# Two masked groups of a chain in one visit over four PSUM banks, and a matrix product cut to 96 rows and columns

## The chip, the cores and the metric

The kernel runs on one core of one Trainium2 chip. The metric is the device time of one execution in microseconds, from runs on the chip. A profile is one further execution, recorded by the hardware profiler; its span runs from the first to the last instruction of the program.

## The reference

One hybrid decoder layer in float32, with 256 tokens of width 2048: a SwiGLU feed-forward, a mixer (sliding-window attention beside RWKV-7 time mixing), cross-attention into a memory of 256 rows, a second feed-forward and a final RMSNorm. What is changed lies in the time mixing. For each of 16 heads of width 64 it is a recurrence over the tokens:

```python
def step(S, inp):
    r_t, w_t, k_t, v_t, a_t, b_t = inp
    sa = jnp.einsum('bhij,bhj->bhi', S, a_t)
    S = S * w_t[:, :, None, :] + sa[..., None] * b_t[:, :, None, :] + v_t[..., None] * k_t[:, :, None, :]
    return S, jnp.einsum('bhij,bhj->bhi', S, r_t)
```

A step needs the state that the step before left. The kernel works instead in chunks of 128 tokens: within a chunk it solves a triangular system, and between the two chunks it hands on the state.

## The kernel before

Weight products fill TensorE from the first to the last microsecond. A weight tile of 128x512 is split into a high and a low part (`hi` on ScalarE, line 365; `lo` on VectorE, line 366), and each product is three matmuls of 512 columns (lines 442 to 444). The two parts are made up to two items ahead (`AHEAD`); an item is 12 matmuls in the mixer.

All other work of the mixer is written as Python generators in an `Interleave`. After each group of six product matmuls `bg.tick()` lets every active generator emit its next step, up to its `yield`. So the steps of a chain stand in the queues of the engines between the weight products, one step per tick; `idle(n)` is n ticks in which a generator emits nothing. The framework then orders the instructions and sets all semaphores: an instruction that finds no free buffer is put later, and an instruction may go ahead of one that was emitted earlier.

The generator `pairs(h, q)` is the chain. Each of its four instances (h and q are 0 or 1) carries two pairs of heads through the two chunks c = 0 and 1, and at most two instances run at a time. In order of steps:

- `masked` (line 1315) multiplies keys, removal keys and receptances (lines 1326 and 1327; the two heads of a pair stand on partitions 0 to 63 and 64 to 127, each goes to a bank of its own) and applies a triangular mask on VectorE (line 1332). It is called three times: for the first two kinds of c = 0 (`mk`), one tick later for the third kind of both chunks (`later`), and after `sa` for the first two kinds of c = 1 (`mk_next`).
- `u` (line 1363) is the right side of the system; N (line 1378) is the product of two precomputed parts of its matrix: `x` holds the inverses of the four 32x32 diagonal blocks, `rr` what lies below those blocks. `nt` is N copied to SBUF (line 1383).
- `stage` (line 1387) does one product and its copy to SBUF. `v0` is x times u; then three products with N: `v1` = v0 + N v0, `w` = N v1, `sa` = v1 + N w. They share one bank `vb`, and `v1` and `sa` add onto what `v0` left there. `rr` holds nothing in rows 0 to 31 and nothing in columns 96 to 127; so the first 32 columns of `nt` and its rows 96 to 127 are zero.
- The output `y` and, for c = 0, the state `s0`.

PSUM has eight banks: three `acc` for the weight products, three `mm` and two `tr`. In this part of the kernel `mm` holds `vb` of each chain and, for a short time, the transposes `bk`; `tr` holds the masked products, `u`, N, `y`, and the transposes and sums of other generators (`finish`, `values`, `shifted`).

POOL (GpSimd) fills and loads `x` and `rr` (`inverse_blocks`, lines 1299 to 1305), loads `g2` in `finish` (lines 1467 to 1469) and stores `gr` (line 1524).

Of the kernel before, what the change touches and what calls it, by code (L numbers as in the profile page):

```python
# [15 lines left out]
P = 128  # L16
# [120 lines left out]
def decoder_layer(ctx: ExitStack, tc: tile.TileContext, a: dict, out: bass.AP):  # L137
    nc = tc.nc
    act, dve, pool, pe = nc.scalar, nc.vector, nc.gpsimd, nc.tensor
# [26 lines left out]
    def tr():  # L166
        return ps.tile([P, 512], F32, tag="tr", name="tr", bufs=2)
# [5 lines left out]
    def idle(n):  # L173
        for _ in range(n):
            yield
# [94 lines left out]
    for entry in weight_plan(a):  # L270
# [4 lines left out]
        w, k0, nk, c0, n = entry  # L275
# [5 lines left out]
        for k in range(k0, k0 + nk, 2 * KU):  # L281
            u = len(units)
# [528 lines left out]
    with tc.tile_pool(name="f1", bufs=1, reuse_waits="tile") as sp:  # L811
        aligned(sp)
        at["pool"] = sp
        x = sp.tile([P, 2, D], F32, name="x")
# [58 lines left out]
    with tc.tile_pool(name="mx", bufs=1, reuse_waits="tile") as sp:  # L873
# [3 lines left out]
        def t4(name, shape=(P, 4, T), dt=F32):  # L877
            return sp.tile(list(shape), dt, tag="t4", name=name, bufs=N4)
# [427 lines left out]
            xb[h, c] = x, r  # L1306

        rows = [slice(64 * e, 64 * e + 64) for e in range(2)]
        ek = dict(skip_group_check=True)
        yq = {}  # L1310

        def small(name, tag="sm", bufs=6):
            return sp.tile([P, 2, P], F32, tag=tag, name=name, bufs=bufs)

        def masked(h, js, which):


            sides = ((aa[h], at_[h]), (aa[h], rt[h]), (bt[h], rt[h]))
            b = [tr() for _ in range(2)]
            for i, (m, c) in enumerate(which):  # L1320
                cs_ = slice(c * P, (c + 1) * P)
                x1, x2 = sides[m]
                for k, j in enumerate(js):
                    o = (2 * i + k) * P
                    for e, r in enumerate(rows):
                        pe.matmul(  # L1326
                            b[e][:, o : o + P], x1[r, j, cs_], x2[r, j, cs_], start=True, stop=True
                        )
            t = t4("mk", (P, 2, 4, P))
            mask = mask3[:, :2] if which[0][0] == 0 else mask3[:, 1:]  # L1330
            for e in range(2):
                dve.tensor_tensor(
                    t[:, e].rearrange("p (m k) t -> p m k t", m=2),
                    b[e][:].rearrange("p (m k t) -> p m k t", m=2, k=2),
                    mask.unsqueeze(2).to_broadcast([P, 2, 2, P]), ALU.mult,
                )
            return t

        def pairs(h, q):
            yield from wait_for("inverse")  # L1340
            yield from wait_for(f"ready{h}")
            js = (2 * q, 2 * q + 1)
            y = yq[h, q] = sp.tile([P, 2, T], F32, tag="yq", name="yq", bufs=3)
            if q == 0:
                for c in range(2):
                    inverse_blocks(h, c)

            yield from idle(4 + 4 * q)
            ah, bh, kh, rh = at_[h], bt[h], aa[h], rt[h]
            s0 = later = None  # L1350
            for c in range(2):
                cs_ = slice(c * P, (c + 1) * P)
                if c == 0:
                    mk = masked(h, js, ((0, 0), (1, 0)))
                    yield
                    later = masked(h, js, ((2, 0), (2, 1)))
                    yield
                vp = [vtok[h][:, c, j * P : (j + 1) * P] for j in js]
                x, rr = xb[h, c]
                b = tr()  # L1360
                for k, j in enumerate(js):
                    for e, r in enumerate(rows):
                        pe.matmul(
                            b[:, k * P : (k + 1) * P][:, r], mk[:, e, k, :], vp[k][:, r],
                            start=k + e == 0, stop=c == 0, **ek,
                        )
                    if c:
                        pe.matmul(
                            b[:, k * P : (k + 1) * P], ah[:, j, cs_], s0[:, k, :], start=False,
                            stop=True, **ek,  # L1370
                        )
                u = small("u")
                act.copy(u[:], b[:, : 2 * P].rearrange("p (k f) -> p k f", k=2))
                b = tr()
                for k, j in enumerate(js):
                    for e in range(2):
                        o = (2 * k + e) * P
                        pe.matmul(
                            b[:, o : o + P], rr[:, 4 * e + j, :], x[:, 4 * e + j, :],
                            start=o == 0, stop=True, **ek,  # L1380
                        )
                nt = sp.tile([P, 4, P], F32, tag="nt", name="nt", bufs=2)
                act.copy(nt[:], b[:].rearrange("p (k t) -> p k t", k=4))
                yield
                vb = mm()

                def stage(lhs, rhs, o, first, name):
                    for k in range(2):
                        for e, r in enumerate(rows):
                            pe.matmul(  # L1390
                                vb[:, (o + k) * P : (o + k + 1) * P][:, r], lhs(k, e), rhs[:, k, r],
                                start=first and k + e == 0, stop=True, **ek,
                            )
                    s = small(name)
                    act.copy(
                        s[:], vb[:, o * P : (o + 2) * P].rearrange("p (k f) -> p k f", k=2)
                    )
                    return s

                v0 = stage(lambda k, e: x[:, 4 * e + js[k], :], u, 0, True, "v0")  # L1400
                if c == 0:
                    b = mm()
                    for k, j in enumerate(js):
                        for i, z in enumerate((bh, kh)):
                            o = (2 * k + i) * P
                            pe.transpose(b[:, o : o + P], z[:, j, cs_], ident[:])
                    bk = sp.tile([P, 4, P], F32, tag="bk", name="bk", bufs=2)
                    act.copy(bk[:], b[:].rearrange("p (x f) -> p x f", x=4))
                yield
                v1 = stage(lambda k, e: nt[:, 2 * k + e, :], v0, 0, False, "v1")  # L1410
                yield
                w = stage(lambda k, e: nt[:, 2 * k + e, :], v1, 2, False, "w")
                yield
                sa = stage(lambda k, e: nt[:, 2 * k + e, :], w, 0, False, "sa")
                yield
                if c == 0:
                    mk_next = masked(h, js, ((0, 1), (1, 1)))
                    yield
                b = tr()
                if c:  # L1420
                    for k, j in enumerate(js):
                        pe.matmul(
                            b[:, k * P : (k + 1) * P], s0[:, k, :], rh[:, j, cs_], start=k == 0,
                            stop=False, **ek,
                        )
                for k in range(2):
                    o = slice(k * P, (k + 1) * P)
                    for e, r in enumerate(rows):
                        pe.matmul(
                            b[r, o], vp[k][:, r], mk[:, e, 2 + k, :], start=c + k == 0, stop=False,  # L1430
                            **ek,
                        )
                    for e, r in enumerate(rows):
                        pe.matmul(
                            b[r, o], sa[:, k, r], later[:, e, 2 * c + k, :], start=False, stop=True,
                            **ek,
                        )
                if c == 0:
                    for k in range(2):
                        bs = b[:, (2 + k) * P : (3 + k) * P]  # L1440
                        pe.matmul(bs, bk[:, 2 * k, :], sa[:, k, :], start=False, stop=False, **ek)
                        pe.matmul(bs, bk[:, 2 * k + 1, :], vp[k], start=False, stop=True, **ek)
                act.copy(y[:, :, cs_], b[:, : 2 * P].rearrange("p (k t) -> p k t", k=2))
                if c == 0:
                    s0 = small("s0", "s0", 2)
                    for k, j in enumerate(js):
                        dve.scalar_tensor_tensor(
                            s0[:, k, :], b[:, (2 + k) * P : (3 + k) * P], dec[h][:, j : j + 1],
                            bdup[:], ALU.mult, ALU.mult,
                        )  # L1450
                    mk = mk_next
                yield
            for j in js:
                bg.seen.add(f"y{4 * h + j}")
# [104 lines left out]
        for n in range(4):  # L1559
            s = t4("x2", (P, 2, 512))  # L1560
# [193 lines left out]
```

## Time and profile before

| | |
|---|---|
| time, median of 3 runs | 2233.55 us (2233.27 to 2233.90) |
| the profiled execution's own time | 2234.97 us |
| its span, first to last instruction | 2233.2 us |
| granted TensorE clock | 0.999 |
| TensorE busy (matmuls; weight loads) | 2218.3 us; 1825.6 us |
| VectorE, ScalarE, GpSimd busy | 1828.1, 1248.2, 116.6 us |
| HBM | 208 GB/s over the span |
| the changed code runs | 1099 to 1252 us |

In the lines of the profile PE is TensorE's matmuls, PEld its weight loads, DVE is VectorE, ACT ScalarE, POOL GpSimd. A group shows its line of the program, engine, operation, output and inputs, for TensorE rows*columns of the array, then the shape of the operand that is read, and the count. One fp32 product of the program is two matmuls and two weight loads in the trace. Matmuls overlap, so the spacing of their starts says more than how long one lasts. In lists of one line's instructions the three numbers are shortest, median and longest, in ns. In the chain of waits and the timeline the first number is the start in us and the second the length.

### The profile page before, as it was taken

What the parts mean: (1) busy time and instruction counts of PE and PEld (TensorE: products, weight loads), DVE (VectorE), ACT (ScalarE), POOL (GpSimd) and SP (SyncE); (2) the same over time, 40 slices, a digit from 0 to 9 for tenths busy, and PEclk for the clock granted to TensorE, in tenths of its full rate; (3) what the DMA queues carried; (4) which work ended last, traced back from release to release, by engine and by line L of the source; (5) the groups of instructions that cost most, each with busy time, mean ns of one, the idle gap of its engine ahead of it and who ended that gap; (6) DMA issues with size and microseconds to landing.
All of it is one profiled execution on the core that took longest, in us unless ns stands there. A gap on an engine that the chain in (4) does not pass through costs nothing.

```text
span 2233.2 us, 28140 instructions
## 1 busy us (share of the span) xinstructions
PE 2218.3 (99%) x10520; PEld 1825.6 (82%) x10520; DVE 1828.1 (82%) x2366; ACT 1248.2 (56%) x1626; POOL 116.6 (5%) x181
## 2 busy tenths in 40 slices
PE   9999999999999999999999999999999999999998
PEld 7888888888888877788888888888888888888876
DVE  7999989898989477877657656547999999999997
ACT  7555555555556468544444546556665565655654
POOL 0000000000001001200221030001000000000000
PEclk9999999999999999999999999999999999999999
DMA  8565566556556545677768688658575576556563
GB/s 303 193 211 199 189 208 201 194 189 212 202 189 199 173 134 153 188 236 208 225 202 277 200 262 282 188 160 279 195 251 194 193 245 207 203 208 220 198 240 137
DMA packets 231561, 466.02 MB, mean 209 GB/s; under 512 B 15521, under 2 KB 17921, under 8 KB 231425
## 3 DMA queue, kind: packets, MB, share of 16 engines
q1 hardware_dynamic: 222256, 438.08, 59.3%
q0 software_dynamic: 7648, 23.52, 3.4%
q10 hardware_dynamic: 1520, 2.63, 0.3%
q8 instruction: 82, 1.34, 0.3%
q14 instruction: 55, 0.44, 0.1%
HBM read 440.49 MB, written 23.59 MB: 208 GB/s over the span
## 4 chain that ended last, share of the span: by engine, by line
PE 91%; DVE 4%; DMA 3%; issue 1%; ACT 1%; SPq 0%; POOL 0%; POOLq 0%; ACTq 0%; DVEq 0%
PE acc L442 18%; PE acc L443 18%; PE acc L444 18%; PE mm L442 8%; PE mm L443 8%; PE mm L444 8%; PE tr L443 2%; PE tr L630 2%; PE tr L442 2%; PE tr L444 2%; DVE lo L366 2%; PE mm L1390 1%; DMA raw<-in_ffn_w_up_dram 1%; PE tr L1326 1%; PE mm L949 0%
## 5 line engine op out<-in xcount | busy, mean ns | idle before, releaser
L365 ACT CAST hi<-raw 128x1024 fp32r<-128x1024 f32 (+1 forms) x768 | 754.9, 993 | 685.6 <-PE acc L444 500.9
L366 DVE TENSOR_TENSOR lo<-raw,hi 128x1024 fp32r<-128x1024 f32 (+1 forms) x768 | 882.5, 1152 | 298.7 <-ACT hi L365 296.2
L442 PE MATMUL acc<-hi,xhi 128*128 128x512 f32 (+1 forms) x1134 | 446.9, 395 | 2.3 <-ACT hi L365 0.8
L443 PE MATMUL acc<-lo,xhi 128*128 128x512 f32 (+1 forms) x1134 | 440.5, 389 | 0.8 <-DVE lo L366 0.8
L444 PE MATMUL acc<-hi,xlo 128*128 128x512 f32 (+1 forms) x1134 | 440.2, 388 | 0.0
L442 PEld LDWEIGHTS acc<-hi,xhi 128*128 128x128 f32 x1134 | 212.8, 188 | 49.4 <-issue 3.7
L443 PEld LDWEIGHTS acc<-lo,xhi 128*128 128x128 f32 x1134 | 213.1, 188 | 44.9 <-DVE lo L366 2.1
L444 PEld LDWEIGHTS acc<-hi,xlo 128*128 128x128 f32 x1134 | 213.0, 188 | 44.2 <-issue 1.3
L373 ACT CAST thi<-raw 128x1024 fp32r<-128x1024 f32 x192 | 200.3, 1052 | 75.2 <-DVE raw L396 50.6
L374 DVE TENSOR_TENSOR tlo<-raw,thi 128x1024 fp32r<-128x1024 f32 x192 | 232.1, 1217 | 0.8 <-ACT thi L373 0.2
L442 PE MATMUL mm<-hi,xhi 128*128 128x512 f32 x402 | 156.6, 389 | 0.0
L443 PE MATMUL mm<-lo,xhi 128*128 128x512 f32 x402 | 156.5, 389 | 0.0
L444 PE MATMUL mm<-hi,xlo 128*128 128x512 f32 x402 | 156.4, 389 | 0.0
L444 PE MATMUL acc<-hi,hlo 128*128 128x512 f32 x372 | 145.4, 391 | 0.0
L443 PE MATMUL acc<-lo,hhi 128*128 128x512 f32 x372 | 145.3, 391 | 0.0
L442 PE MATMUL acc<-hi,hhi 128*128 128x512 f32 x372 | 145.0, 390 | 0.0
L442 PEld LDWEIGHTS mm<-hi,xhi 128*128 128x128 f32 x402 | 75.5, 188 | 16.3 <-ACT hi L365 0.5
L443 PEld LDWEIGHTS mm<-lo,xhi 128*128 128x128 f32 x402 | 75.5, 188 | 15.8
L444 PEld LDWEIGHTS mm<-hi,xlo 128*128 128x128 f32 x402 | 75.5, 188 | 15.7
L443 PEld LDWEIGHTS acc<-lo,hhi 128*128 128x128 f32 x372 | 69.8, 188 | 14.4
L444 PEld LDWEIGHTS acc<-hi,hlo 128*128 128x128 f32 x372 | 69.9, 188 | 14.1
L442 PEld LDWEIGHTS acc<-hi,hhi 128*128 128x128 f32 x372 | 69.9, 188 | 14.1
(400 smaller groups left out, 3548.7 us busy)
## 6 DMA issues: line engine op xcount, KB each, us to landing
raw<-in_ffn_w_down_dram SPq DMA_DIRECT2D x88, 1024.0 KB, 5.2
raw<-in_ffn_w_gate_dram SPq DMA_DIRECT2D x84, 1024.0 KB, 5.2
raw<-in_ffn_w_up_dram SPq DMA_DIRECT2D x78, 1024.0 KB, 6.1
raw<-in_w_in_dram SPq DMA_DIRECT2D x136, 512.0 KB, 3.7
raw<-in_w_out_dram SPq DMA_DIRECT2D x32, 512.0 KB, 4.8
raw<-sums SPq DMA_DIRECT2D x20, 512.0 KB, 6.3
raw<-in_w_proj_attn_dram SPq DMA_DIRECT2D x16, 512.0 KB, 4.3
raw<-in_w_proj_rwkv_dram SPq DMA_DIRECT2D x16, 512.0 KB, 6.0
```

What stands on the lines that cost most here:

```text
L365: at["hi"] = act.copy(hi[:, s], raw[:, s])
L366: at["lo"] = dve.tensor_tensor(lo[:, s], raw[:, s], f32(hi[:, s]), ALU.subtract)
L373: act.copy(hi[:], v[:])
L374: dve.tensor_tensor(lo[:], v[:], f32(hi[:]), ALU.subtract)
L442: pe.matmul(o, xh, hi, start=first, stop=False, **how)
L443: pe.matmul(o, xh, lo, start=False, stop=False, **how)
L444: pe.matmul(o, xl, hi, start=False, stop=last, **how)
L630: pe.transpose(b[:, o : o + P], tok[:, t, col : col + P], ident[:])
L1326: pe.matmul(b[e][:, o : o + P], x1[r, j, cs_], x2[r, j, cs_], start=True, stop=True)
L1390: pe.matmul(vb[:, (o + k) * P : (o + k + 1) * P][:, r], lhs(k, e), rhs[:, k, r], start=first and k + e == 0, stop=True, **ek,)
```

## The change

`masked` is split into `scores`, which does the matmuls into banks of a given ring, and `masked`, which applies the mask. For c = 0 the first and the second group are now emitted in the same step: the first into the two `tr` banks, the second into two `mm` banks; the four masks follow, and two idle ticks stand where the two steps were. The third group is as before.

N is computed for 96 rows (weights `rr` in 96 columns) and 96 columns (`x` without its first 32); the first 32 columns of `nt`, which the copy no longer writes, are set to zero by a memset on POOL. The products with N (`lower`) contract over 96 partitions in place of 128, and `w` is computed for 96 output rows only, since what follows reads no more of it.

```diff
@@ -1306,17 +1306,16 @@
             xb[h, c] = x, r
 
         rows = [slice(64 * e, 64 * e + 64) for e in range(2)]
+        low = slice(0, 96)
         ek = dict(skip_group_check=True)
         yq = {}
 
         def small(name, tag="sm", bufs=6):
             return sp.tile([P, 2, P], F32, tag=tag, name=name, bufs=bufs)
 
-        def masked(h, js, which):
-
-
+        def scores(h, js, which, bank):
             sides = ((aa[h], at_[h]), (aa[h], rt[h]), (bt[h], rt[h]))
-            b = [tr() for _ in range(2)]
+            b = [bank() for _ in range(2)]
             for i, (m, c) in enumerate(which):
                 cs_ = slice(c * P, (c + 1) * P)
                 x1, x2 = sides[m]
@@ -1326,8 +1325,10 @@
                         pe.matmul(
                             b[e][:, o : o + P], x1[r, j, cs_], x2[r, j, cs_], start=True, stop=True
                         )
+            return b
+
+        def masked(b, mask):
             t = t4("mk", (P, 2, 4, P))
-            mask = mask3[:, :2] if which[0][0] == 0 else mask3[:, 1:]
             for e in range(2):
                 dve.tensor_tensor(
                     t[:, e].rearrange("p (m k) t -> p m k t", m=2),
@@ -1351,10 +1352,11 @@
             for c in range(2):
                 cs_ = slice(c * P, (c + 1) * P)
                 if c == 0:
-                    mk = masked(h, js, ((0, 0), (1, 0)))
-                    yield
-                    later = masked(h, js, ((2, 0), (2, 1)))
-                    yield
+                    first = scores(h, js, ((0, 0), (1, 0)), tr)
+                    second = scores(h, js, ((2, 0), (2, 1)), mm)
+                    mk = masked(first, mask3[:, :2])
+                    later = masked(second, mask3[:, 1:])
+                    yield from idle(2)
                 vp = [vtok[h][:, c, j * P : (j + 1) * P] for j in js]
                 x, rr = xb[h, c]
                 b = tr()
@@ -1376,28 +1378,38 @@
                     for e in range(2):
                         o = (2 * k + e) * P
                         pe.matmul(
-                            b[:, o : o + P], rr[:, 4 * e + j, :], x[:, 4 * e + j, :],
-                            start=o == 0, stop=True, **ek,
+                            b[low, o + 32 : o + P], rr[:, 4 * e + j, low],
+                            x[:, 4 * e + j, 32:], start=o == 0, stop=True, **ek,
                         )
                 nt = sp.tile([P, 4, P], F32, tag="nt", name="nt", bufs=2)
-                act.copy(nt[:], b[:].rearrange("p (k t) -> p k t", k=4))
+                pool.memset(nt[low, :, :32], 0.0)
+                act.copy(
+                    nt[low, :, 32:], b[low].rearrange("p (k t) -> p k t", k=4)[:, :, 32:]
+                )
                 yield
                 vb = mm()
 
-                def stage(lhs, rhs, o, first, name):
+                def stage(lhs, rhs, o, first, name, to=slice(0, P)):
                     for k in range(2):
                         for e, r in enumerate(rows):
                             pe.matmul(
-                                vb[:, (o + k) * P : (o + k + 1) * P][:, r], lhs(k, e), rhs[:, k, r],
-                                start=first and k + e == 0, stop=True, **ek,
+                                vb[to, (o + k) * P : (o + k + 1) * P][:, r], lhs(k, e)[:, to],
+                                rhs(k)[:, r], start=first and k + e == 0, stop=True, **ek,
                             )
                     s = small(name)
                     act.copy(
-                        s[:], vb[:, o * P : (o + 2) * P].rearrange("p (k f) -> p k f", k=2)
+                        s[to], vb[to, o * P : (o + 2) * P].rearrange("p (k f) -> p k f", k=2)
                     )
                     return s
 
-                v0 = stage(lambda k, e: x[:, 4 * e + js[k], :], u, 0, True, "v0")
+                def lower(v, o, name, to=slice(0, P)):
+                    return stage(
+                        lambda k, e: nt[low, 2 * k + e, :], lambda k: v[low, k], o, False, name, to
+                    )
+
+                v0 = stage(
+                    lambda k, e: x[:, 4 * e + js[k], :], lambda k: u[:, k], 0, True, "v0"
+                )
                 if c == 0:
                     b = mm()
                     for k, j in enumerate(js):
@@ -1407,14 +1419,14 @@
                     bk = sp.tile([P, 4, P], F32, tag="bk", name="bk", bufs=2)
                     act.copy(bk[:], b[:].rearrange("p (x f) -> p x f", x=4))
                 yield
-                v1 = stage(lambda k, e: nt[:, 2 * k + e, :], v0, 0, False, "v1")
-                yield
-                w = stage(lambda k, e: nt[:, 2 * k + e, :], v1, 2, False, "w")
-                yield
-                sa = stage(lambda k, e: nt[:, 2 * k + e, :], w, 0, False, "sa")
+                v1 = lower(v0, 0, "v1")
+                yield
+                w = lower(v1, 2, "w", low)
+                yield
+                sa = lower(w, 0, "sa")
                 yield
                 if c == 0:
-                    mk_next = masked(h, js, ((0, 1), (1, 1)))
+                    mk_next = masked(scores(h, js, ((0, 1), (1, 1)), tr), mask3[:, :2])
                     yield
                 b = tr()
                 if c:
```

## The prediction

> **What bounds the kernel now.** I read the page first (busy shares, then the chain that ended last), then one window around the changed code, then single lines in it.
>
> ```profile
> span 2233.2 us, 28140 instructions
> ...
> PE 2218.3 (99%) x10520; PEld 1825.6 (82%) x10520; DVE 1828.1 (82%) x2366; ACT 1248.2 (56%) x1626; POOL 116.6 (5%) x181
> ...
> PE 91%; DVE 4%; DMA 3%; issue 1%; ACT 1%; SPq 0%; POOL 0%; POOLq 0%; ACTq 0%; DVEq 0%
> ```
>
> TensorE (PE) is busy 99% of the span and carries 91% of the chain that ended last. Every instruction queues behind the one before it there, so a microsecond taken from TensorE anywhere shortens the run by a microsecond, if nothing else runs dry. The changed code runs in one place, the stretch from 1099 to 1252 us, where the four `pairs` chains are mixed into the weight products. The windows view gives it (busy time and count of PE, PEld, DVE, ACT and POOL, then granted clock, DMA share, GB/s):
>
> ```profile
> 1099.00:1252.00 153.00, 152.59 (x1117) 132.34 (x1117) 97.59 (x134) 70.23 (x115) 29.32 (x49) 1.00 0.75 240
> ```
>
> PE is full at full clock, DVE is at 64%, ACT at 46%, POOL at 19%. The view of waits of the same stretch says who stands ahead of whom (total us, times, longest):
>
> ```profile
> POOL g L1467 <- DVE gh L1485: 54.3, 2, 39.1
> DVE lo L366 <- ACT hi L365: 31.1, 16, 5.3
> POOL grd L1524 <- ACT gr L1523: 25.0, 2, 21.5
> ACT hi L365 <- PE acc L444: 23.2, 19, 2.3
> ```
>
> The weight splits `hi` and `lo` wait for TensorE to free their buffers, 19 times of 23, so they are made ahead of need. POOL waits long and often, and nobody here waits for POOL. So the stretch is bound by the number and the pitch of TensorE's instructions, and by the few places where it waits.
>
> **The change, part by part.** One fp32 product of the program is two TensorE instructions, so N (L1378) is 64 instructions, and the second product with N, which makes `w`, is half of the 128 in the group `mm<-v,nt` of L1390, 64 more.
>
> ```profile
> L1378 PEld LDWEIGHTS tr<-xb,rb x64: 187/192/192, 1110.6 to 1237.8; 128*128 128x128 f32 x64
> L1378 PE MATMUL tr<-xb,rb x64: 272/275/328, 1110.8 to 1237.9; 128*128 128x128 f32 x64
> L1378 PEldq EVENT_SEMAPHORE  x16: 51/51/1717, 1109.5 to 1207.7; - x16
> L1390 PE MATMUL mm<-v,nt x128: 217/275/275, 1116.4 to 1245.2; 128*128 128x64 f32 x128
> L1429 PEld LDWEIGHTS tr<-mk,vtok x64: 132/136/137, 1132.9 to 1251.0; 128*64 128x64 f32 x64
> ```
>
> ```profile
> 1110.82 1.05 PE L1378 MATMUL tr<-xb,rb 128*128 128x128 f32 x8
> 1111.63 0.47 PE L443 MATMUL acc<-lo,xhi 128*128 128x512 f32 x1
> 1111.94 0.39 PE L444 MATMUL acc<-hi,xlo 128*128 128x512 f32 x1
> ...
> 1112.87 1.00 PE L1390 MATMUL mm<-u,xb 128*128 128x64 f32 x8
> 1113.70 0.28 PE L1406 MATMUL mm<-ident,kk 128*128 128x128 f32 x1
> ```
>
> *N in 96 columns and 96 rows.* In the timeline eight instructions of N take 0.81 us (1110.82 to 1111.63) with 128 moving columns; eight of L1390 take 0.83 us (1112.87 to 1113.70) with 64. Half the moving columns buy nothing, so the weight load sets the pitch. A load of 128 columns lasts 192 ns, one of 64 columns 137 ns: 55 ns for 64 columns, 27.5 ns for the 32 that go. N loses them in the load and in the moving operand alike (a matmul's shortest duration falls from 272 to 217 ns over 64 columns, the same 55 ns). 64 x 27.5 ns = **-1.8 us**. Ends: 0, if 96 columns cost what 128 do, and -1.8; no row has 96 columns, and I take the straight line because both ends of it are measured.
>
> *`w` in 96 columns.* The load shrinks by the same 32 columns and the moving operand is 64 wide as before; the load sets the pitch, so again 64 x 27.5 ns = **-1.8 us**, ends as before. The 96 rows of v1, `w` and `sa` (contraction over 96 partitions) save nothing: loads of 64 rows in L1326 and of 128 rows differ by a few ns (182 to 188 against 187 to 192, below). ACT's copies of N and `w` get smaller or stay, beside TensorE's products: 0.
>
> *The second group in banks of its own.* Before, a chain's second masked group (L1326, x16) takes the two `tr` banks that the first has just filled, and TensorE waits until DVE has read them out. The chain of waits shows the four second groups (start, us), and after them three stretches in which only one bank was free and half a group was issued:
>
> ```profile
> 1106.54 1.75 PE tr L1326 x16
> 1120.95 1.09 PE tr L1326 x16
> 1179.96 1.42 PE tr L1326 x16
> 1199.82 1.09 PE tr L1326 x8
> 1203.68 1.08 PE tr L1326 x8
> 1206.37 1.08 PE tr L1326 x8
> 1210.62 1.83 PE tr L1326 x15
> ```
>
> An undisturbed group takes 1.09. The others are 0.66, 0.33 and 0.74 over it: **-1.7 us** if the `mm` banks are free. They should be: three `mm` banks, of which the other chain holds one (`vb`) when this chain starts, and its `bk` bank was read a tick earlier. Ends: 0 (the wait comes back at another instruction) and -3.3, since the three half groups take 1.08 for 8, where 16 should; without the second group in the `tr` ring they might come whole, 3 x 0.54 = 1.6 more.
>
> *One visit in place of two.* A group of L1326 uses 64 rows of the array, two products side by side; going in and out of that costs time:
>
> ```profile
> L1326 PEld LDWEIGHTS tr<-rt,kk x64: 182/188/188, 1106.5 to 1212.1; 64*128 64x128 f32 x64
> 1103.14 0.39 PE L443 MATMUL acc<-lo,xhi 128*128 128x512 f32 x1
> 1103.37 0.39 PE L444 MATMUL acc<-hi,xlo 128*128 128x512 f32 x1
> 1103.69 0.71 PE L1326 MATMUL tr<-at,aa 64*128 64x128 f32 x8
> 1104.23 0.61 PE L1326 MATMUL tr<-rt,aa 64*128 64x128 f32 x8
> 1104.78 0.50 PE L442 MATMUL acc<-hi,xhi 128*128 128x512 f32 x1
> 1105.12 0.39 PE L443 MATMUL acc<-lo,xhi 128*128 128x512 f32 x1
> ```
>
> ```profile
> 1151.03 0.39 PE L1434 MATMUL tr<-mk,sa 128*64 128x128 f32 x4
> 1151.24 0.39 PE L1429 MATMUL tr<-mk,vtok 128*64 128x128 f32 x4
> ```
>
> Two products follow each other at 0.23 us; from the last product to the group it is 0.32 (+0.09) and from the first product after it to the next 0.34 (+0.11). Inside, two side by side take 0.11 when running (four in 0.21 at 1151.03), so eight such twos are 0.88 of the 1.09: +0.21. A visit costs 0.20 to 0.41. Some of these groups stand beside blocks of the other chain, whose exit is paid anyway, so I take 0.3; four visits fewer: **-1.2 us**, ends -0.8 and -1.6. The Trainium skill, "TensorEngine Tiling (Array Packing)", Key Properties, says that changing the tiling mode drains TensorE, and gives no price; here the trace agrees, at these 0.20 to 0.41 us.
>
> *What is added.* DVE gets four masks in a row instead of two and two, and POOL eight small memsets:
>
> ```profile
> L1332 DVE TENSOR_TENSOR mk<-tr,mask x24: 676/682/692, 1105.8 to 1232.3; 128x512 f32<-128x512 f32 x24
> L1299 POOL MEMSET xb<- x4: 957/974/979, 1091.2 to 1167.8; 128x1024 f32 x4
> L1021 POOL MEMSET p<- x14: 96/102/105, 727.2 to 1091.1; 128x2 f32 x14
> ```
>
> The two later masks push a `lo` split by 2 x 0.68 = 1.4 us. A split is made while at least one further item of 12 products (12 x 0.23 = 2.7 us) is ready, and 16 of 23 splits found DVE waiting for ACT: 0; if that cover is gone once in the crowded third part around 1200 us, +1.4. A memset of 128 elements lies between 0.10 (2 elements) and 0.12 us (an eighth of 974 ns), on an engine that is busy 19%. But behind it v1 waits, and behind v1 all of TensorE. Ahead of it on POOL can stand the long waits: `grd` waits for a sigmoid of a product that is itself behind v1, so the memset can't be queued behind that one in a program that moves at all; the others (`g`, up to 39.1 us) began when POOL had run far ahead. I take 0, and +2 as the far end (one memset late by one or two ticks). For one more semaphore on TensorE before each v1, 51 ns as in the third row of L1378: 8 x 51 ns = **+0.4 us**.
>
> Sum: -1.8 - 1.8 - 1.7 - 1.2 + 0.4 = **-6.1 us**. It is made against the profiled execution (2234.97 us, its span 2233.2); that one is 1.4 us above the median, and I carry the difference over unchanged: 2233.55 - 6.1 = **2227.4 us**. About 0.2% of the time, 4.5 us, is what a measurement of this kernel can tell from no change.
>
> **The rivals.** *96 columns cost what 128 do.* Both -1.8 go, -2.5 remains: 2231.0. For it: no row shows a width between 64 and 128. Against it: durations scale between these two on both paths.
>
> *The wait comes back.* The second groups find their banks, but the order in the crowded stretch around 1200 us changes and TensorE waits for masks, for `tr` banks or for a late `lo` instead; -1.7 and most of -1.2 go: -3.2 with the added 0.4, 2230.3. For it: the half groups, which show that the ring of two `tr` banks stays short for the first groups too. This is also the case in which the banks do not do what the change says.
>
> *A 96 is a mode of its own, the slower end.* N, v1, `w` and `sa` are 8 groups each, 32 in all, and each has a 96 in rows or in columns. If TensorE drains before and after such a group, each pays 0.30 us (0.09 before it and 0.21 inside, as above): 32 x 0.30 = +9.6. If 96 then also gains nothing in columns, -2.5 + 9.6 = +7.1: 2240.6. It decides from 0.08 us for a group in that case (2.5 / 32), from 0.19 (6.1 / 32) with the columns' gain. The same section of the Trainium skill names 128, 64 and 32 as sizes of a tile and no 96. For it: L1326 and L1429 pay at each change of size. Against it: a 96 needs the whole array in both directions, as 128 does, and 64 or 32 do not.
>
> **How the numbers follow.** The forecast 0.50; 96 as 128: 0.18; the wait comes back: 0.17; a mode of its own: 0.15. The two in the middle are within 0.2%, so faster 0.50, same 0.35, slower 0.15. The range goes down to 2224.5 (the half groups whole, -1.6, and the larger price of a visit, -0.4, and about 1 us for a later order of the queues) and up to 2236.0: 2231.0 with +1.4 from DVE, +2 from POOL and the rest of the visits' -1.2 lost. It leaves out the mode of its own, 0.15.
>
> **What would show it.** Right: loads of L1378's successor and of `w` at about 165 ns (halfway between 192 and 137) and eight of them in about 0.6 us; four groups of 32 masked instructions in about 2 us without a gap; no wait on POOL before v1. Wrong: loads of 96 columns at 192 ns; 0.3 us gaps before each group of v1; a wait of PE for POOL `nt`; half groups in the new `mm` banks; a wait for `lo` right after four masks.

## The result and the profile after

The changed kernel takes 2228.82 us in the median of 9 runs, the kernel before 2234.13 us beside it; the ratio is 0.9974 with a 95% interval of 0.9965 to 0.9983. One of the 9 runs was slow, 4512.34 us, and is left out of the ratio; the median of the other 8 is 2228.58. In a later set of runs it was 2228.76 against 2234.62 us, 0.9973 (0.9963 to 0.9984). So it is faster, by 5.6 and 5.9 us; the forecast was 6.1. Its profiled execution took 2228.33 us, with a span 6.8 us shorter than before. From the page of the kernel after, the lines that answer to the first fence of the prediction:

```profile
span 2226.4 us, 28168 instructions
...
PE 2211.5 (99%) x10520; PEld 1821.2 (82%) x10520; DVE 1828.8 (82%) x2366; ACT 1247.6 (56%) x1626; POOL 118.0 (5%) x189
...
PE 92%; DVE 4%; issue 1%; DMA 1%; ACT 1%; SPq 0%; POOLq 0%; POOL 0%; DVEq 0%; ACTq 0%
```

TensorE still has 10520 matmuls and is still what bounds the run; it is busy 6.8 us less, as much as the spans differ. POOL has eight instructions more. The windows view of the chains' stretch, now from 1095 to 1245 us, and the waits there:

```profile
1095.00:1245.00 150.00, 148.95 (x1134) 130.07 (x1132) 100.89 (x138) 70.00 (x115) 34.44 (x61) 1.00 0.78 250
```

```profile
POOL nt L1385 <- PE mm L1395: 69.4, 5, 24.6
ACT hi L365 <- PE acc L444: 35.6, 22, 4.1
```

PE remains full at full clock. The new memset `nt` waits up to 24.6 us for its buffer, and in that view no engine waits for POOL: each memset ends 17 us or more before its v1 starts. The splits `hi` still wait for TensorE's buffers (35.6 us in this window), so the four masks in a row have not used up that cover.

The rows of N (now line 1380) and of v1 and `w` (line 1395; the first form of the last row is v1, the second `w`) give the new loads:

```profile
L1380 PEld LDWEIGHTS tr<-xb,rb x64: 163/165/165, 1109.2 to 1231.5; 128*96 128x96 f32 x64
L1380 PE MATMUL tr<-xb,rb x64: 246/248/275, 1109.3 to 1231.5; 128*96 128x96 f32 x64
L1395 PEld LDWEIGHTS mm<-v,nt x128: 161/176/192, 1114.8 to 1238.6; 96*128 96x128 f32 x64, 96*96 96x96 f32 x64
```

A load of 96 columns takes 165 ns, the straight line between 192 and 137. In the timeline of the kernel after eight instructions of N go from 1178.92 to 1179.55 us, and eight of `w` from 1186.22 to 1186.85, 0.63 us each where it was 0.81. For `w` that is the distance of the first two rows, from the timeline of the kernel before; the others are from the kernel after:

```profile
1190.18 1.00 PE L1390 MATMUL mm<-v,nt 128*128 128x64 f32 x8
1190.98 0.48 PE L444 MATMUL acc<-hi,xlo 128*128 128x512 f32 x1
...
1178.92 0.84 PE L1380 MATMUL tr<-xb,rb 128*96 128x96 f32 x8
1179.55 0.47 PE L443 MATMUL acc<-lo,xhi 128*128 128x512 f32 x1
...
1186.22 0.81 PE L1395 MATMUL mm<-v,nt 96*96 96x64 f32 x8
1186.85 0.48 PE L442 MATMUL acc<-hi,xhi 128*128 128x512 f32 x1
...
1188.32 1.00 PE L1395 MATMUL mm<-w,nt 96*128 96x64 f32 x8
1189.13 0.48 PE L1505 MATMUL tr<-xr,gh 128*128 128x256 f32 x2
```

The last two rows are `sa` and what follows it, with 96 rows and 128 columns: 0.81 us for eight, as with 128 rows.

The masked groups in the chain of waits of the kernel after (`tr` is the first group or `mk_next`, `mm` the second):

```profile
1103.66 1.09 PE tr L1325 x16
1104.75 0.89 PE mm L1325 x16
1115.94 1.10 PE tr L1325 x16
1117.03 0.89 PE mm L1325 x16
...
1191.71 1.09 PE tr L1325 x8
1194.40 0.53 PE mm L1325 x5
1195.04 0.68 PE tr L1325 x7
1198.05 0.97 PE tr L1325 x7
1199.13 0.45 PE mm L1325 x7
1200.24 1.08 PE tr L1325 x8
```

In the first two chains 32 instructions run in one piece, 1.09 and 0.89 us. In the fourth, which meets the third chain's `mk_next`, first groups and `mk_next` are still issued in halves of 8 in about 1.09 us, and pieces of the second group fill in between. In the third chain a wait for DVE now stands before the products with the gate's weights in `finish` (line 1505), which want a `tr` bank right behind the two groups (timeline of the kernel after):

```profile
1172.21 1.06 PE L1325 MATMUL mm<-rt,kk 64*128 64x128 f32 x16
1174.00 0.50 PE L1505 MATMUL tr<-xr,gh 128*128 128x256 f32 x2 [0.73 <-DVE mk L1333]
```

What frees that bank is the first of the four masks, which DVE starts at 1173.26 only; ahead of it DVE makes a `lo` from 1171.53 and an `sg` from 1172.66. The two masks that were a step later before come behind it, from 1174.46, so this is not their price.

To see where TensorE's time went I added up, in both traces, the distances from each matmul's start to the next one's, between two points that both kernels have: the last matmul of line 1195 and the first product with `yr`. The stretch is 343.0 us before and 336.5 after; a second execution of the changed kernel (run "again" below) gives 336.5 too, so it tells more than the medians of whole runs, and it is given for the experiments as well.

| us of TensorE | before | after | difference |
|---|---|---|---|
| N | 7.04 | 5.13 | -1.9 |
| v1 and `w` | 13.55 | 11.99 | -1.6 |
| masked products | 17.11 | 15.29 | -1.8 |
| weight products | 251.86 | 251.08 | -0.8 |
| all else | 53.46 | 53.03 | -0.4 |

A wait, or the time that entering and leaving a masked group costs, is counted here with the instruction before it; the weight products' -0.8 are such distances at least in part. In the run with the banks alone (below) N takes 6.74 us with its columns as before, so the columns brought 1.6 of N's 1.9.

### The profile page after: what moved, and what is told of

Read it like the earlier page. It is cut to its first block, busy times and chain, and to the rows that moved or that the text cites. A ratio compares the mean times of both kernels' runs of the same rounds, so it can differ in the third digit from the quotient of the medians.

```text
span 2226.4 us, 28168 instructions
## 1 busy us (share of the span) xinstructions
PE 2211.5 (99%) x10520; PEld 1821.2 (82%) x10520; DVE 1828.8 (82%) x2366; ACT 1247.6 (56%) x1626; POOL 118.0 (5%) x189
## 4 chain that ended last, share of the span: by engine, by line
PE 92%; DVE 4%; issue 1%; DMA 1%; ACT 1%; SPq 0%; POOLq 0%; POOL 0%; DVEq 0%; ACTq 0%
PE acc L442 19%; PE acc L443 18%; PE acc L444 18%; PE mm L444 8%; PE mm L443 8%; PE mm L442 8%; PE tr L630 2%; PE tr L443 2%; PE tr L442 2%; PE tr L444 2%; DVE lo L366 2%; PE mm L1395 1%; DMA raw<-in_ffn_w_up_dram 1%; PE mm L949 0%; ACT hi L365 0%
```

## The experiments

Theory: the two parts work independently; in N and `w` the slower of load and stream sets the pitch, both at 1.2 columns per ns (the prediction's 32 columns in 27.5 ns); the second groups gain because they need not wait for DVE to read their banks, and a little because of one visit less. Rivals: the columns are only shorter on paper, or the merged step alone does it, or the gain is the order's. Differences below are between medians of runs on one chip; intervals are those of the ratio to the kernel before. Each diff is against the changed kernel.

### The columns alone

```diff
-                    first = scores(h, js, ((0, 0), (1, 0)), tr)
-                    second = scores(h, js, ((2, 0), (2, 1)), mm)
-                    mk = masked(first, mask3[:, :2])
-                    later = masked(second, mask3[:, 1:])
-                    yield from idle(2)
+                    mk = masked(scores(h, js, ((0, 0), (1, 0)), tr), mask3[:, :2])
+                    yield
+                    later = masked(scores(h, js, ((2, 0), (2, 1)), tr), mask3[:, 1:])
+                    yield
```

> The kernel before with the 96 rows and columns alone; the masked groups stay in two steps on the tr banks. Theory (loads and moving columns set the pitch, each part's gain is its own): N and w are eight instructions in 0.62 us in place of 0.81, 2 x 8 x 8 x 0.19/8 = -3.0 to -3.5 us against before, and the second masked groups still take 1.4 to 1.9 us where they wait. Rival (the gain comes from the merged groups and their order, the columns only look shorter): within 1 us of before.

2231.90 us against 2234.67: -2.8 us, ratio 0.9986 (0.9977 to 0.9995). In its chain of waits the second groups wait as before:

```profile
1107.10 1.75 PE tr L1325 x16
1121.15 1.09 PE tr L1325 x16
1178.97 1.42 PE tr L1325 x16
1208.97 1.77 PE tr L1325 x16
```

The rival falls: the columns bring 2.8 us by themselves, a little less than the 3.0 to 3.5 expected. The stretch is 3.2 us shorter than before (339.8).

### The banks alone

```diff
-        low = slice(0, 96)
+        low = slice(0, 128)
 ...
-                            b[low, o + 32 : o + P], rr[:, 4 * e + j, low],
-                            x[:, 4 * e + j, 32:], start=o == 0, stop=True, **ek,
+                            b[low, o : o + P], rr[:, 4 * e + j, low],
+                            x[:, 4 * e + j, :], start=o == 0, stop=True, **ek,
 ...
-                pool.memset(nt[low, :, :32], 0.0)
                 act.copy(
-                    nt[low, :, 32:], b[low].rearrange("p (k t) -> p k t", k=4)[:, :, 32:]
+                    nt[low], b[low].rearrange("p (k t) -> p k t", k=4)
                 )
```

> The kernel before with the masked groups merged alone; N and w keep 128 rows and columns, no memset. Theory: -2 to -3 us against before, N stays at 0.81 us for eight. Rival (the waits only move to masks or tr banks once the columns' time is not there): within 1 us of before. If the two parts are independent, this gain and that of the columns alone add up to that of the whole change, -5.3 to -6.5 us, within 1 us.

2231.43 us against 2234.67: -3.2 us, 0.9986 (0.9977 to 0.9995), slightly over the range. -2.8 and -3.2 make -6.0, and the whole change had -5.9 in the later set: the parts add up. In the stretch (339.6 here) it is -3.2 and -3.4 against -6.5.

### A load of 96 columns and a stream of 128

```diff
-                            b[low, o + 32 : o + P], rr[:, 4 * e + j, low],
-                            x[:, 4 * e + j, 32:], start=o == 0, stop=True, **ek,
+                            b[low, o : o + P], rr[:, 4 * e + j, low],
+                            x[:, 4 * e + j, :], start=o == 0, stop=True, **ek,
 ...
-                pool.memset(nt[low, :, :32], 0.0)
                 act.copy(
-                    nt[low, :, 32:], b[low].rearrange("p (k t) -> p k t", k=4)[:, :, 32:]
+                    nt[low], b[low].rearrange("p (k t) -> p k t", k=4)
                 )
```

> The whole change, but N streams all 128 columns of x (no memset): its load is 96 columns, its moving operand 128; w is as in the change. Theory of the prediction (the pitch is the slower of load and stream, 1.2 columns per ns each): eight instructions of N at 0.85 to 0.9 us, all of N's 1.5 to 1.9 us lost against the changed kernel. Rival (the load alone sets the pitch): eight in 0.62 us, time as the changed kernel.

2229.75 us, 0.9976 (0.9967 to 0.9986): 4.9 us below before, 1.0 short of the changed kernel's 5.9. Its timeline:

```profile
1179.91 1.04 PE L1380 MATMUL tr<-xb,rb 128*96 128x128 f32 x8
1180.70 0.48 PE L443 MATMUL acc<-lo,xhi 128*128 128x512 f32 x1
```

Eight instructions of N take 0.79 us, not 0.63: with 128 columns streaming, the shorter load buys next to nothing. That is lower than the 0.85 to 0.9 expected, but the rival's 0.62 is far off. The sum for N in the stretch is 6.51 us, 1.4 above the changed kernel. Expected was a loss of 1.5 to 1.9 us in time; the 1.0 is less.

### A stream of 96 columns and loads of 128

```diff
-        low = slice(0, 96)
+        low = slice(0, 128)
```

> The whole change, but all weight loads have 128 columns and all contractions 128 rows: N streams 96 columns only, w is computed in full. Theory: eight instructions of N and of w at 0.81 us each, as before, since the load of 128 columns sets the pitch; 3.0 to 3.5 us more than the changed kernel, the same as the merged groups alone to 0.5 us. Rival (the moving columns count): N at 0.62 us, 1.5 us more than the changed kernel.

2231.47 us, 0.9986 (0.9977 to 0.9995), the same as the banks alone (2231.43). Its timeline, N and then `w`:

```profile
1180.39 1.03 PE L1380 MATMUL tr<-xb,rb 128*128 128x96 f32 x8
1181.20 0.48 PE L443 MATMUL acc<-lo,xhi 128*128 128x512 f32 x1
...
1187.86 1.00 PE L1395 MATMUL mm<-v,nt 128*128 128x64 f32 x8
1188.66 0.48 PE L442 MATMUL acc<-hi,xhi 128*128 128x512 f32 x1
...
1190.13 1.00 PE L1395 MATMUL mm<-w,nt 128*128 128x64 f32 x8
1190.94 0.48 PE L1505 MATMUL tr<-xr,gh 128*128 128x256 f32 x2
```

N takes 0.81 us, `w` 0.80: the stream of 96 alone buys nothing. N gains only when both shrink; `w`, with a stream of 64, gains from the load alone. `sa` takes 0.81 us with 128 rows, and 0.81 with 96 in the kernel after: the rows neither gain nor cost.

### The changed kernel again, as a base

> The changed kernel itself, on the chip of the other three of this set, as their base: 5.3 to 6.5 us less than before.

2228.76 us against 2234.62, as told above, with a stretch of 336.5 us.

### Four banks, two steps

```diff
-                    first = scores(h, js, ((0, 0), (1, 0)), tr)
-                    second = scores(h, js, ((2, 0), (2, 1)), mm)
-                    mk = masked(first, mask3[:, :2])
-                    later = masked(second, mask3[:, 1:])
-                    yield from idle(2)
+                    mk = masked(scores(h, js, ((0, 0), (1, 0)), tr), mask3[:, :2])
+                    yield
+                    later = masked(scores(h, js, ((2, 0), (2, 1)), mm), mask3[:, 1:])
+                    yield
```

> The changed kernel, but the second masked group is again emitted one step later, still into the mm banks: four banks, two visits. Theory (the banks take away the wait, the common step takes away a visit of 0.2 to 0.41 us): the second groups take 1.09 to 1.10 us each in place of 1.09 to 1.83, and the time lies 0.8 to 1.6 us above the changed kernel. Rival (the visit costs nothing by itself, all of the gain is the wait): within 0.4 us of the changed kernel. Second rival (the common step is all of it): the waits stay, 2.5 us or more above it.

2229.21 us, 0.9975 (0.9966 to 0.9985): 0.45 us above the changed kernel, between what the first rival (within 0.4) and the theory (0.8 to 1.6) gave, and the ranges of the runs overlap (2227.72 to 2230.02 against 2228.03 to 2229.09). The stretch decides better: 337.4 us, 0.9 above the changed kernel. The second groups of the first two chains stand alone, without a wait, so the second rival falls (timeline, first chain):

```profile
1105.90 0.40 PE L444 MATMUL acc<-hi,xlo 128*128 128x512 f32 x1
1106.23 1.16 PE L1325 MATMUL mm<-rt,kk 64*128 64x128 f32 x16
1107.32 0.50 PE L442 MATMUL acc<-hi,xhi 128*128 128x512 f32 x1
1107.66 0.39 PE L443 MATMUL acc<-lo,xhi 128*128 128x512 f32 x1
```

The group is 0.33 us behind the product ahead of it and the product after it 0.34 us from the next, where two products are 0.23 apart; its 16 instructions take 1.09 us, where they take 0.89 right behind the first group. That makes 0.4 us. The starts of the same weight products in both traces say so too: against the changed kernel this one falls back by 0.42 us at the first chain's groups and by 0.35 at the second's. At the third it loses nothing, because the order put the second group right behind the first although it is emitted a step later:

```profile
1172.46 0.61 PE L1325 MATMUL tr<-rt,aa 64*128 64x128 f32 x8
1172.91 1.06 PE L1325 MATMUL mm<-rt,kk 64*128 64x128 f32 x16
```

At the fourth, where the groups are in pieces, it loses 0.2. So a visit that stands alone costs 0.35 to 0.42 us, and the common step takes away two of them, not four. The banks without the common step bring 2.4 us in the stretch against the columns alone; counted in the same way it is 0.8 in the first chain, nothing in the second, 0.1 in the third, where the new wait of 0.73 us stands against the gain, and 1.5 in the fourth. Of the merge's gain the larger part is the banks'.

### Two banks, one step

```diff
-                    first = scores(h, js, ((0, 0), (1, 0)), tr)
-                    second = scores(h, js, ((2, 0), (2, 1)), mm)
-                    mk = masked(first, mask3[:, :2])
-                    later = masked(second, mask3[:, 1:])
+                    mk = masked(scores(h, js, ((0, 0), (1, 0)), tr), mask3[:, :2])
+                    later = masked(scores(h, js, ((2, 0), (2, 1)), tr), mask3[:, 1:])
```

> The changed kernel, but both masked groups take the two tr banks, emitted in one step: one step, two banks. Theory (the banks decide): the second group can only start when DVE has read the first, so waits of 0.3 us and more come back before the second groups, often as half groups of 8 instructions in 1.09 us; 1.5 to 4 us above the changed kernel. Rival (emitting them together is enough, the order fills the wait with products): within 0.5 us of it.

2232.42 us, 0.9991 (0.9982 to 1.0): 3.7 us above the changed kernel, within the theory's range. The waits are back in its chain of waits, in the second chain too, which had none before:

```profile
1106.78 1.75 PE tr L1325 x15
1119.69 1.63 PE tr L1325 x15
1177.12 1.42 PE tr L1325 x16
```

So the common step without the banks is worth nothing. It isn't a common visit either: in the first chain the first group ends at 1105.09 us, and weight products stand between it and the second.

### The fourth chain four ticks earlier

```diff
-            yield from idle(4 + 4 * q)
+            yield from idle(4 + 4 * q * (1 - h))
```

> The changed kernel, but the fourth chain (h = 1, q = 1) starts four ticks earlier, so that it stands four ticks behind the third, as the second stands behind the first; before, it stood eight behind, and its first group met the third chain's masks for the second chunk on the tr banks. Theory (the half groups around 1190 to 1201 us come from that meeting): no half groups, masked instructions down from 15.3 to about 13.5 us in the stretch, 1 to 2 us below the changed kernel. Rival (some other holder of the tr banks, such as the norm's sums, makes the halves): half groups elsewhere, within 0.5 us of the changed kernel.

2226.16 us, 0.9963 (0.9949 to 0.9977): 2.6 us below the changed kernel, the best of all, and its slowest run (2226.61) is below the fastest of the changed kernel (2228.03). The groups of the last two chains in its chain of waits:

```profile
1184.30 1.19 PE tr L1325 x14
1185.72 0.89 PE mm L1325 x14
1195.07 1.42 PE tr L1325 x16
1211.87 1.09 PE tr L1325 x16
```

The half groups are gone, and the masked products in the stretch take 13.77 us in place of 15.29, -1.5. So the halves came from the meeting of the fourth chain's first group with the third chain's `mk_next`. The weight products take 0.9 us less (250.17 against 251.08 in the stretch), some small pieces a little more; the stretch as a whole is 2.1 us shorter (334.4). What is left of the 2.6 us was not split further.

### The same start on the kernel before

The same edit, on the kernel before.

> The kernel before, with the earlier start of the fourth chain alone (four ticks behind the third). Theory (the half groups come from the meeting of the fourth chain's first group with the third chain's masks, whatever the banks of the second groups): 1.5 to 2.6 us less than before. Rival (the earlier start pays only once the second groups have left the tr banks, since they would now meet other users of that ring): within 0.7 us of before, or slower.

2233.32 against 2234.45 us: -1.1 us, 0.9995 (0.9986 to 1.0004), which the runs can't tell from no change; the stretch is 0.9 us shorter (342.1). The expected 1.5 to 2.6 us are not there. The halves do not go; they take other groups, among them the second group itself (chain of waits):

```profile
1188.72 1.08 PE tr L1326 x8
1190.70 1.09 PE tr L1326 x8
1193.52 1.09 PE tr L1326 x8
1196.20 1.09 PE tr L1326 x8
```

The theory of that run is wrong in "whatever the banks": the earlier start pays when the second groups have left the `tr` ring, and about 1 us at most before. What holds the banks in this run was not traced further.

## Why the prediction was right

The forecast was 2227.4 us in a range of 2224.5 to 2236.0; measured were 2228.82 and 2228.76. Faster by over 0.2% was given 0.50, and that is what came, by a small margin (0.26 and 0.27%).

- **N in 96 columns and rows**, forecast -1.8: -1.9 in the stretch's sum, of which the columns have 1.6. The load of 165 ns was forecast to the nanosecond, but the distance of two instructions is not the load's length: eight went from 0.81 to 0.63 us, 22 ns for each where 27.5 were taken. That the load sets the pitch was half of the reason: the two runs with only one side cut show that load and stream both have to shrink, as they did in the change.
- **`w` in 96 columns**, forecast -1.8: -1.6 for v1 and `w` together; v1 changes nothing. The size is off for the same reason. Together the columns alone gave 2.8 us in time and 3.2 in the stretch, 0.8 and 0.4 less than the two terms.
- **The second group in banks of its own**, forecast -1.7, was too small: -2.4 in the stretch. The term took 0.66, 0.33 and 0.74 us from the first, third and fourth chain; they gave 0.8, 0.1 and 1.5. The third chain lost its wait and got a new one. Why the fourth gave twice what its second group had over 1.09 us was not traced. The halves, which the prediction held possible as a further -1.6, stayed: 8 instructions in 1.08 us at 1200.24 after the change.
- **One visit in place of two**, forecast -1.2 with -0.8 as its near end, was too large: -0.9 in the stretch, -0.45 in the medians. A visit alone costs 0.35 to 0.42 us, the upper end of the 0.20 to 0.41 that the prediction read, where it took 0.3. The step that failed is the count: the common step takes away two visits and not four, since the third chain's groups stand together as soon as they have banks, and the fourth's come in pieces with it or without it. The drain at a change of tiling mode that the Trainium skill names ("TensorEngine Tiling (Array Packing)", Key Properties) is in the trace, at that price for going in and out.
- **What is added**, forecast +0.4 with ends at +1.4 from DVE and +2 from POOL: nothing of it is seen as a term. No engine waits for the memset. The 0.73 us before the gate's products in the third chain are the wait in another place that the second rival named, at a small part of its price; TensorE waits there for the first of the four masks, so the two added ones did not make it.
- **The sum.** In the stretch the columns, the banks and the visit make -3.2, -2.4 and -0.9, which is -6.5; forecast were -3.6, -1.7, -1.2 and +0.4. That -6.1 came so near is in part luck: one term too small stands against two too large and an added one that is not seen.
- **The rivals.** *96 columns cost what 128 do* falls by eight instructions in 0.63 us. *The wait comes back* holds for that one place. *A 96 is a mode of its own* falls: blocks of `96*96` and `96*128` run at 0.63 and 0.81 us for eight and follow a weight product at 0.23 us as blocks of `128*128` do, and `sa` in 128 rows is no faster. (The sizes of a tile that the prediction took from the Trainium skill stand in that page's Available Configurations.)

## What to carry to other kernels

Where small fp32 products sit between large ones on a full TensorE, look first at which of weight load and stream sets their pitch; here cutting the other bought next to nothing, and 96 rows of the contraction in place of 128 bought nothing at all. Take the price from the distance of the starts, not from the length of a load. When the second of two groups waits for the first one's banks, give it other banks: putting both into one step without that brought the waits back. Count what the order makes of a change and not what the program says: two of four visits went. And after a ring is relieved, try the schedule again: a start four ticks earlier, worth 1 us or less before, brought 2.6 us more.

## What was not expected of the hardware

A memset on POOL of 96x4x32 elements in four strided pieces took 0.20 us (201 to 223 ns in the row below), where 0.10 to 0.12 was estimated from a tiny and a large one; it did not matter.

```profile
L1385 POOL MEMSET nt<- x8: 201/202/223, 727.1 to 1217.3; 96x128 f32 x8
```
